# A two-layer hybrid attention network: the value products of four blocks of queries as one group on TensorE

## The chip, the cores and the metric

The kernel runs on one core of one Trainium2 chip. The metric is device time in microseconds of one execution, the median of several runs. The profile is one execution on the same kind of chip, recorded by the hardware profiler. PE is TensorE (matmuls and transposes), DVE is VectorE, ACT is ScalarE, POOL is GpSimd, SP is the engine whose queue issues most of the loads and stores.

## The reference, cut to what matters

The network has two layers over 2048 tokens of width 1024, in float32. The change lies in the second layer ("odd"), which has twelve heads of sliding-window attention with a sink, in three groups that share keys and values, and four heads that attend to a memory of 256 tokens. Each head has 64 features.

```python
def _sliding_window_attention(q, k, v, sinks):
    ...
    def one_block(bi):
        qi = lax.dynamic_slice_in_dim(q, bi * BLOCK, BLOCK, axis=1)
        kb = lax.dynamic_slice_in_dim(kp, bi * BLOCK, 2 * BLOCK, axis=1)
        vb = lax.dynamic_slice_in_dim(vp, bi * BLOCK, 2 * BLOCK, axis=1)
        s = jnp.einsum('bqhgd,bkhd->bhgqk', qi, kb, preferred_element_type=jnp.float32) * scale
        ...
        s = jnp.where(band, s, NEG_BIG)
        m = jnp.maximum(jnp.max(s, axis=-1, keepdims=True), sink)
        p = jnp.exp(s - m)
        w = p / (jnp.sum(p, axis=-1, keepdims=True) + jnp.exp(sink - m))
        return jnp.einsum('bhgqk,bkhd->bqhgd', w.astype(vb.dtype), vb)

def _odd_layer(x, mem, positions, w_in, w_memkv, sinks, w_out, ln_g, ln_b):
    ...
    mixed = jnp.concatenate([c_o, mem_o], axis=-1)
    y = (mixed * jax.nn.silu(gate)) @ w_out
    return _layer_norm(DEEPNORM_ALPHA * x + y, ln_g, ln_b)
```

BLOCK is 128: a block of 128 queries sees its own 128 keys and the 128 before them.

## The kernel before

The work runs in stages: the first layer's projections, its stick-breaking attention, its differential attention, the joining output projection and norm, the second layer's keys, values and gates (`layer2_kv`, `gates`), the second layer's queries and attention (`layer2`), and its output projection and norm (`out_proj`). The change lies in `layer2`.

There, features come in eight tiles `f` of 128 (two heads each; 0 to 5 are the sliding window's, 6 and 7 the memory's) and tokens in four chunks `t` of 512. A pair (f, t) is a chunk of work `i`, 32 in all; each has four blocks of 128 queries. One block of a chunk is a unit `u`, 128 in all. The loop over steps `u` writes several stages of different units side by side:

- the scores of unit u (`swa_scores` or `mem_scores`): four matmuls into a PSUM bank `z` (three of them). Behind them, off PE, comes the softmax: for the sliding window two DVE reductions that add the mask and take the maximum (L1143), a DVE copy of the sinks (L1145), two ACT exponentials with their sums (L1147), a DVE reciprocal (L1148), and the scaling of one head on DVE (L1154) and of the other on ACT (L1152). For the memory these are L484, L487, L489 and L493.
- a quarter of the projection of later queries, six matmuls of 512 columns (`fill`; `psmm`). The finished projection goes through ACT, DVE and POOL (L1116 to L1121, L1102, L1103) to become the next queries.
- the value products of unit u - 5 (`swa_values` or `mem_values`): four matmuls, each shown as two records of 128 by 64, that write a block's 128 columns of the one bank `pv`, the first head to its partitions 0 to 63 and the second to 64 to 127. After a chunk's fourth block DVE multiplies the bank by the chunk's gates (L1362), tile `sl`, and a store takes it to DRAM (`m2`).
- the four transposes of the softmax weights of unit u - 3 (`swa_turn`, `mem_turn`; `pstp`), which ACT or DVE copies from PSUM to a tile `wT` (L122, L124 in `evac`, through `tblocks`).

Only TensorE's instructions keep the order in which they are written (`PinnedCore(nc, self.tc, ("tensor",))`). What DVE, ACT, POOL and SP do, and in which order, is set by a planner that lays the program on a modelled timeline: each engine takes the earliest written instruction that is ready there. On the chip each queue is then kept in that order. A tag of a pool (`wT`, `sl`, `pv`) has a fixed number of buffers, and a new tile waits until the one that had its place is no longer used.

At the step's end, the loads of the next chunk's values and gates are written (`load_v`); keys and tables of angles come in the middle (`load_k`, `load_cs`). At chunk 29 the weights of the output projection are loaded and split in two parts (`load_wo`; L969 on ACT, L971 on POOL).

Line 56 is the helper that records every pinned instruction, so PE's instructions are told apart by their tiles; line 112 is the helper that issues loads and stores.

Of the kernel before, what the change touches and what calls it, by code (L numbers as in the profile page):

```python
# [15 lines left out]
S = 2048  # L16
D = 1024
P = 128
NB = S // P
TC = 512  # L20
# [25 lines left out]
class Pinned:  # L46
    """An engine whose instructions stay in the order in which they are written."""
# [18 lines left out]
class Net:  # L66
# [15 lines left out]
    @contextmanager  # L82
    def phase(self, bufs, banks, side="left"):
        """Pools for one phase; SBUF slots and PSUM banks by tag."""
        with ExitStack() as ctx:
            layer = {k: (n, ctx.enter_context(self.tc.tile_pool(name=self.nm("p" + k), bufs=1, side=side, reuse_waits="tile")))
                     for k, n in bufs.items()}
            if banks:
                ps = ctx.enter_context(self.tc.tile_pool(name=self.nm("pp"), bufs=1, space=bass.MemoryType.PSUM, reuse_waits="tile"))
                layer.update({"ps" + k: (n, ps) for k, n in banks.items()})  # L90
            self.layers.append(layer)
            yield
            self.layers.remove(layer)
# [20 lines left out]
    def turn(self, key, pattern):  # L114
        """The next letter of a repeated pattern: which engine takes this one."""
        k = self.turns.get(key, 0)
        self.turns[key] = k + 1
        return pattern[k % len(pattern)]
# [8 lines left out]
    def consts(self):  # L127
        nc, sb = self.nc, self.sb
# [4 lines left out]
        # nothing, then what is after the query (a column further on: at it or after it)  # L133
# [12 lines left out]
        # -lambda on every partition  # L146
# [26 lines left out]
    def rope_tables(self, k, sink):  # L173
        """cos and sin of the positions' angles, in chunks of 512: sink(chunk, cos, sin)."""
        nc = self.nc
        for t in range(NT):
            posi = self.t("c2", I32)
            self.dma(posi, self.i["pos"][t * TC:(t + 1) * TC].partition_broadcast(P))
            ang = self.t("c2")
            nc.vector.tensor_copy(ang, posi)  # L180
            nc.vector.tensor_scalar_mul(ang, ang, self.freq[:, k:k + 1])
            n = self.t("c2")
            nc.vector.tensor_scalar(n, ang, 1.0 / TWO_PI, MAGIC, ALU.mult, ALU.add)
            nc.vector.tensor_scalar_add(n, n, -MAGIC)
            for c in (C1, C2, C3):
                nc.vector.scalar_tensor_tensor(ang, n, -c, ang, ALU.mult, ALU.add)
            nc.vector.tensor_scalar(ang, ang, math.pi, -math.pi, ALU.min, ALU.max)
            nc.scalar.activation(n, ang, AF.Abs)
            sink(t, n, ang)
            yield  # L190

# [1 line left out]
    def wtile(self, src):  # L193
        """A [P, 8, 128] tile of weights, as two parts."""
        w, (fill,) = self.wtile_steps(src, 1, self.nc.gpsimd)
        fill()
        return w
# [21 lines left out]
    def load_x(self, between):  # L219
        """x transposed, [tc][half] -> (hi, lo) of [P, 4, 512]."""  # L220
        nc = self.nc
# [21 lines left out]
    def proj_t(self, w, t):  # L243
        """[128 features, 512 tokens] of chunk t."""
        return self.proj_side([w], t)[0]

    def proj_side(self, ws, t):
        """The same for several tiles of weights side by side."""
# [8 lines left out]
    def spill_parts(self, ps, dst, t, scale=None):  # L257
        """ps (times a power of two) in two parts to dst [2, P, S]."""
# [112 lines left out]
    def rope_all(self):  # L371
        """Both layers' tables to DRAM, a chunk of one at each next()."""
# [13 lines left out]
    def vtile(self, g):  # L386
        """Weights of 256 columns of the two attentions' values, as two parts of each half."""
# [9 lines left out]
    def values(self, g, ws, side):  # L397
        """256 columns of the two attentions' values, token by token."""
# [19 lines left out]
    def dup_parts(self, hi, lo, src, hh):  # L418
        """Half hh of src's partitions, its two parts in both halves of hi and lo."""
# [13 lines left out]
    def memkv(self, W, mem, keep):  # L433
        """Memory keys of each pair of heads and all values, a weight tile at each next()."""
# [35 lines left out]
    def tblocks(self, blocks, pattern="AV"):  # L470
        """Up to four [P, P] blocks transposed, in SBUF."""
# [8 lines left out]
    def softmax_pair(self, z, e, n0, sink=False):  # L480
        """z [P, 2, 256] -> e, normalised; columns from n0 on; the first is the sink's."""
# [13 lines left out]
    def mem_scores(self, qs, qcol, mk):  # L495
        """One block of queries, heads 2f and 2f+1 over the memory."""
# [20 lines left out]
    def load_qstack(self, src, t):  # L517
        """[P = two copies of 64, 2 heads, 2 parts, 512]."""
# [9 lines left out]
    def load_sb(self, p):  # L528
        """A pair of heads' keys and values and the last chunk's queries."""
# [69 lines left out]
    def differential(self):  # L599
        """Differential attention in three stages, each a unit (two blocks of queries, 17 blocks of  # L600
        keys together, of two heads) behind the one before: scores and exponentials; the mix of the
        two softmaxes; the product with the values. Between them go some feature tiles' share of
        the output projection."""
# [10 lines left out]
        def mixed(a, b):  # L614
            """Two lists evenly mixed, each in its order."""
            order = sorted([((i + 0.5) / len(a), 0, i) for i in range(len(a))] + [((i + 0.5) / len(b), 1, i) for i in range(len(b))])
            return [(a, b)[k][i] for _, k, i in order]
# [56 lines left out]
    def load_dq(self, p, k, h):  # L674
        """Queries of a half of each of the two chunks: units j = 2h and 2h + 1."""
# [7 lines left out]
    def diff_parts(self, unit):  # L683
        """Of the two blocks of queries: their number, the chunk's, the place in it, the keys, the
        first column in a row."""
# [4 lines left out]
    def diff_scores(self, unit, rows):  # L690
        """For each head and component the steps of its scores, and those of the exponentials."""
# [56 lines left out]
    def diff_mix(self, unit, rows):  # L748
        """Steps by beat."""
# [72 lines left out]
    def diff_norm(self, p, t, s0, pv, tail):  # L822
        """rms norm over each head's 64, scaled by the first sum; the rest of its steps to tail."""
# [42 lines left out]
    def filler(self):  # L866
        """alpha x and the share of the output projection of the feature tiles known before the
        differential attention; lists of steps."""
# [60 lines left out]
    def memory(self, mk, mv):  # L929
        """The first layer's attention over the memory, a block at each next(), to go  # L930
        between other projections."""
# [52 lines left out]
    def out_proj(self, w, msrc, spans, res, alpha, lng, lnb, tbs, ahead):  # L984
        """A block of the output projection and its layer norm at each next()."""
# [50 lines left out]
    def join(self, tail):  # L1036
        """The rest of the first layer's output projection, its norm, x of the second layer
        transposed in two parts, and its first gates; the steps in tail go between."""
# [60 lines left out]
    def qstack_head(self, qs, src, hh, eng):  # L1099
        """The two parts of head hh's queries (half of src's partitions), one on top of the other."""  # L1100
# [4 lines left out]
    def qstack_from(self, src, eng):  # L1105
        """[P = two parts of 64, 2 heads, 512] of a tile of two heads' queries (in SBUF)."""
# [22 lines left out]
    def swa_scores(self, qb, head, qs, qcol, ks):  # L1129
        """Heads head and head+1 over a block of keys and the one before; the first  # L1130
        column of that one is out of every query's window and takes the sink."""
# [37 lines left out]
    def gates(self, W, dst, om=None, m1=None, order=None, ws=None):  # L1169
        """silu of the gates to dst; times what has been attended to m1 where that is known."""  # L1170
# [27 lines left out]
    def layer2_kv(self):  # L1198
        """Keys in two parts and values of each group, to DRAM."""
# [35 lines left out]
    def layer2(self):  # L1235
        """The projections of queries go in quarters between the blocks of the attention, whose
        three stages lie a block or two apart."""
# [3 lines left out]
        wts, qss, sls, es, wTs, pvs, ks, vs, out = {}, {}, {}, {}, {}, {}, {}, {}, []  # L1241
# [94 lines left out]
        for u in range(128 + 5):  # L1336
# [13 lines left out]
            if u >= 5:  # L1350
                i, qi = (u - 5) // 4, (u - 5) % 4
                f, t = order[i]
                if qi == 0:
                    pvs[i] = self.psum("pv")
                if f < 6:
                    v = {t_: vs.get((f, t_)) for t_ in (t - 1, t)}
                    self.swa_values(4 * t + qi, wTs.pop(u - 5), cols[qi], v, pvs[i])
                else:
                    self.mem_values(wTs.pop(u - 5), cols[qi], vs[f], pvs[i])
                if qi == 3:  # L1360
                    mt = sls.pop(i)
                    nc.vector.tensor_mul(mt, pvs.pop(i), mt)  # L1362
                    self.dma(self.m2[f, :, t * TC:(t + 1) * TC], mt, nc.scalar if i > 29 else None)
# [8 lines left out]
    def run(self):  # L1372
# [11 lines left out]
        with self.phase({"c2": 3, "sl": 2}, {}):  # L1384
# [4 lines left out]
            with self.phase({"big": 16}, {}):  # L1389
# [7 lines left out]
                with self.phase({"w": 4, "raw": 1, "cs": 2, "e": 4, "wT": 4, "kc": 2, "qs": 2, "vg": 4},  # L1397
# [78 lines left out]
```

## Time and profile before

| | |
|---|---|
| median of 3 runs | 2660.3 us (2658.35 to 2661.22) |
| the profiled execution (span from first to last instruction) | 2665.1 us |
| PE busy | 2503.5 us, 94% of the span |
| DVE busy | 1656.7 us, 62% |
| ACT busy | 1264.2 us, 47% |
| POOL busy | 1189.9 us, 45% |
| value products of layer 2 (`pspv<-wT,vg`), PE | 1000 records, 83.0 us busy in all |
| steps of the loop in `layer2` | from about 2075 to 2482.6 us of the span |

The profile has no time of the profiled execution but its span, 2665.1 us; that stands 4.8 us over the median of the runs. Matmuls overlap, and their ends are modelled, so a length of a PE row is no cost; the distance from one group's start to the next one's start is.

### The profile page before, as it was taken

What the parts mean: (1) busy time and instruction counts of PE and PEld (TensorE: products, weight loads), DVE (VectorE), ACT (ScalarE), POOL (GpSimd) and SP (SyncE); (2) the same over time, 40 slices, a digit from 0 to 9 for tenths busy, and PEclk for the clock granted to TensorE, in tenths of its full rate; (3) what the DMA queues carried; (4) which work ended last, traced back from release to release, by engine and by line L of the source; (5) the groups of instructions that cost most, each with busy time, mean ns of one, the idle gap of its engine ahead of it and who ended that gap; (6) DMA issues with size and microseconds to landing.
All of it is one profiled execution on the core that took longest, in us unless ns stands there. A gap on an engine that the chain in (4) does not pass through costs nothing. (4 is left out here: it accounts for less than half of the span.)

```text
span 2665.1 us, 42634 instructions
## 1 busy us (share of the span) xinstructions
PE 2503.5 (94%) x15564; PEld 1964.7 (74%) x15564; DVE 1656.7 (62%) x3672; ACT 1264.2 (47%) x2653; POOL 1189.9 (45%) x848
## 2 busy tenths in 40 slices
PE   9899999999989999968877988999999999999998
PEld 7788998888757777646655666678788777777887
DVE  5732223421379999888889878788321667677554
ACT  4532222221167777555665765744121677776200
POOL 1301004730056666465646746764541555535333
PEclk9999999999989999989988988999999999999999
DMA  7643223321842331442523422265332555532541
GB/s 273 212 146 125 70 88 105 137 103 52 203 104 70 82 71 34 99 116 73 127 78 95 108 76 74 70 215 173 88 101 75 162 154 162 152 96 99 194 147 67
DMA packets 199250, 311.60 MB, mean 117 GB/s; under 512 B 17921, under 2 KB 97281, under 8 KB 198529
## 3 DMA queue, kind: packets, MB, share of 16 engines
q1 hardware_dynamic: 198464, 307.83, 39.3%
q8 instruction: 123, 2.02, 0.3%
q10 hardware_dynamic: 576, 1.05, 0.1%
q14 instruction: 87, 0.70, 0.1%
HBM read 204.74 MB, written 104.07 MB: 116 GB/s over the span
## 5 line engine op out<-in xcount | busy, mean ns | idle before, releaser
L56 PE MATMUL psmm<-big,w 128*128 128x512 f32 x1680 | 415.4, 395 | 0.0
L56 PEld LDWEIGHTS psmm<-big,w 128*128 128x128 f32 x1680 | 306.8, 189 | 58.3
L586 POOL TENSOR_TENSOR wb<-wb,row 128x512 f32<-128x512 f32 (+3 forms) x192 | 219.5, 1154 | 136.4 <-DVE row L582 126.9
L582 DVE TENSOR_TENSOR_SCAN row<-psz,row,zero 128x512 f32<-128x512 f32 (+5 forms) x240 | 258.5, 1107 | 31.9 <-ACT psz L579 31.6
L253 PE MATMUL psmm<-big,w 128*128 128x512 f32 x1200 | 275.2, 389 | 0.0
L253 PEld LDWEIGHTS psmm<-big,w 128*128 128x128 f32 x1200 | 225.0, 188 | 47.0 <-issue 0.2
L56 ACT ACTIVATE row<-row,mn 128x2048 f32<-128x2048 f32 (+7 forms) x192 | 229.7, 1201 | 33.6 <-DVE mn L731 33.0
L56 PE MATMUL psmm<-big,mp 128*128 128x512 f32 x1056 | 244.5, 392 | 0.0
L725 DVE TENSOR_SCALAR_CACHE_REDUCE row<-psz 128x512 f32<-128x512 f32 (+1 forms) x324 | 200.9, 640 | 58.4 <-PE psz L56 55.9
L56 PEld LDWEIGHTS psmm<-big,mp 128*128 128x128 f32 x1056 | 198.3, 189 | 41.3 <-issue 0.3
L56 ACT COPY wT<-pstp 128x512 f32<-128x512 f32 (+3 forms) x240 | 121.4, 522 | 169.8 <-PE pstp L56 163.0
L1190 DVE TENSOR_TENSOR c<-psmm,c 128x512 f32<-128x512 f32 x62 | 42.6, 691 | 240.3 <-ACT c L1189 240.3
L592 PE MATMUL pspv<-wT,kv 128*64 128x128 f32 x1632 | 158.1, 287 | 15.4 <-ACT wT L122 15.4
L771 POOL TENSOR_TENSOR row<-row,tiny 128x1536 f32<-128x1536 f32 (+3 forms) x48 | 132.9, 2769 | 83.9 <-DVE tiny L766 78.1
L772 POOL TENSOR_TENSOR row<-row,row 128x1536 f32<-128x1536 f32 (+3 forms) x48 | 163.3, 3408 | 1.9
L208 POOL TENSOR_TENSOR w<-w,w 128x1024 fp32r<-128x1024 f32 x20 | 48.8, 2440 | 255.8 <-ACT w L207 155.4
L56 PE MATMUL psmm<-wo,mp 128*128 128x512 f32 x480 | 155.3, 437 | 3.1 <-ACT mp L56 2.3
L578 ACT ACTIVATE wb<-psz 128x512 f32<-128x512 f32 (+3 forms) x240 | 129.9, 541 | 53.6 <-PE pstp L475 37.2
L778 DVE SCALAR_TENSOR_TENSOR row<-row,tiny,row 128x128 f32<-128x128 f32 (+7 forms) x72 | 153.2, 2154 | 0.5
L573 PE MATMUL psz<-kv,qs 128*128 128x512 f32 (+3 forms) x480 | 150.0, 406 | 2.1 <-DVE row L582 2.0
L592 PEld LDWEIGHTS pspv<-wT,kv 128*64 128x64 f32 x1632 | 106.7, 139 | 60.5 <-issue 20.5
L56 PE MATMUL pstp<-ident,row 128*128 128x128 f32 x816 | 142.0, 297 | 9.7 <-DVE c L860 8.1
(222 smaller groups left out, 5241.6 us busy)
## 6 DMA issues: line engine op xcount, KB each, us to landing
silu<-c SPq DMA_DIRECT2D x54, 256.0 KB, 2.3
sl<-silu SPq DMA_DIRECT2D x54, 256.0 KB, 3.3
qs<-sbq SPq DMA_DIRECT2D x48, 256.0 KB, 5.3
cs<-rope SPq DMA_DIRECT2D x24, 512.0 KB, 4.4
kc<-k SPq DMA_DIRECT2D x36, 320.0 KB, 5.1
w<-in_we_dram SPq DMA_DIRECT2D x20, 512.0 KB, 3.7
raw<-in_wo_dram SPq DMA_DIRECT2D x20, 512.0 KB, 4.0
rx<-in_x_dram SPq DMA_DIRECT2D x32, 256.0 KB, 2.7
```

What stands on the lines that cost most here:

```text
L56: return self.tc.keep_in_program_order(f(*a, **k))
L208: eng.tensor_sub(lo[:, sl], raw[:, sl], hi[:, sl].bitcast(F32))
L253: self.nc.tensor.matmul(ps, w[a][:, c, :], self.xpart(t, c, b), start=(c == k == 0), stop=(c == 7 and k == 2))
L573: nc.tensor.matmul(z[:, :m], qs[:, hh, k, qcol], ks[hh][:, lo:hi], start=(k == 0), stop=(k == 1 and not diag))
L578: nc.scalar.activation(w[:, :m], z[:, :m], AF.Sigmoid, scale=0.125)
L582: nc.vector.tensor_tensor_scan(prr[:, lo + s0 - 1:hi - 1][:, ::-1], z[:, s0:m][:, ::-1], self.zero.to_broadcast([P, m - s0]), prr[:, hi - ...
L586: eng.tensor_mul(w[:, :m], w[:, :m], prr[:, lo:hi])
L592: nc.tensor.matmul(pv[64 * hh:64 * hh + 64, qcol], vp[:, blk, 64 * hh:64 * hh + 64], wT[hh][:, j * P:(j + 1) * P], start=(hi == n and j == ...
L725: nc.vector.tensor_scalar(e[:, col + lo:col + lo + n0], z[:, :n0], -scale, before, ALU.mult, ALU.min, accum_out=acc)
L771: self.nc.gpsimd.tensor_mul(y[:, a:n], y[:, a:n], cf[hh][:, :1].to_broadcast([P, n - a]))
L772: self.nc.gpsimd.tensor_add(x[:, a:n], x[:, a:n], y[:, a:n])
L778: self.nc.vector.scalar_tensor_tensor(x[:, lo:hi], y[:, lo:hi], cf[hh][:, w:w + 1], x[:, lo:hi], ALU.mult, ALU.add)
```

## The change

A chunk's value products are no longer written block by block at four steps, one behind another. They are written together, at every fourth step: at step u, a multiple of four from 8 on, all 16 matmuls (12 where the chunk's first block has half of them) of chunk (u - 8) / 4, that is of units u - 8 to u - 5, then at once the product with the gates and the store. These stood at the same step before. The pool of transposed weights has six tiles and not four, the pool of gates (which the first layer's differential attention uses too) three and not two, and the scratch that is set aside for DMA descriptors is given a size of 2048. The rest of the diff takes out comments and descriptions, at unchanged line numbers.

```diff
-            if u >= 5:
-                i, qi = (u - 5) // 4, (u - 5) % 4
+            if u >= 8 and u % 4 == 0:
+                i = (u - 8) // 4
                 f, t = order[i]
-                if qi == 0:
-                    pvs[i] = self.psum("pv")
-                if f < 6:
-                    v = {t_: vs.get((f, t_)) for t_ in (t - 1, t)}
-                    self.swa_values(4 * t + qi, wTs.pop(u - 5), cols[qi], v, pvs[i])
-                else:
-                    self.mem_values(wTs.pop(u - 5), cols[qi], vs[f], pvs[i])
-                if qi == 3:
-                    mt = sls.pop(i)
-                    nc.vector.tensor_mul(mt, pvs.pop(i), mt)
-                    self.dma(self.m2[f, :, t * TC:(t + 1) * TC], mt, nc.scalar if i > 29 else None)
+                pv = self.psum("pv")
+                for qi in range(4):
+                    if f < 6:
+                        v = {t_: vs.get((f, t_)) for t_ in (t - 1, t)}
+                        self.swa_values(4 * t + qi, wTs.pop(4 * i + qi), cols[qi], v, pv)
+                    else:
+                        self.mem_values(wTs.pop(4 * i + qi), cols[qi], vs[f], pv)
+                mt = sls.pop(i)
+                nc.vector.tensor_mul(mt, pv, mt)
+                self.dma(self.m2[f, :, t * TC:(t + 1) * TC], mt, nc.scalar if i > 29 else None)
...
-        with self.phase({"c2": 3, "sl": 2}, {}):
+        with self.phase({"c2": 3, "sl": 3}, {}):
...
-                with self.phase({"w": 4, "raw": 1, "cs": 2, "e": 4, "wT": 4, "kc": 2, "qs": 2, "vg": 4},
+                with self.phase({"w": 4, "raw": 1, "cs": 2, "e": 4, "wT": 6, "kc": 2, "qs": 2, "vg": 4},
                                 {"mm": 2, "z": 3, "tp": 2, "pv": 1}):
...
-    nc = _bacc.Bacc("TRN2", target_bir_lowering=False, num_devices=1)
+    nc = _bacc.Bacc("TRN2", target_bir_lowering=False, num_devices=1, dynamic_dma_scratch_size=2048)
```

More of the change, by code (lines that the diff above doesn't have):

```diff
@@ L1240, in layer2 @@
         W = self.i["wo"]
-        wts, qss, sls, es, wTs, pvs, ks, vs, out = {}, {}, {}, {}, {}, {}, {}, {}, []
+        wts, qss, sls, es, wTs, ks, vs, out = {}, {}, {}, {}, {}, {}, {}, []
         order = [(f, t) for f in range(7) for t in range(NT)] + [(7, t) for t in (3, 0, 1, 2)]
```

## The prediction

> **What bounds the kernel now.** First the page's span, then the busy table of the second layer's attention (stretch, length, each engine's busy us and instructions, granted clock, DMA share, GB/s).
>
> ```profile
> span 2665.1 us, 42634 instructions
> ```
>
> ```profile
> core 0: us, PE busy (x) PEld busy (x) DVE busy (x) ACT busy (x) POOL busy (x), PEclk, DMA share, GB/s
> 2093.57:2376.84 283.27, 273.78 (x1961) 208.29 (x1959) 198.81 (x814) 208.57 (x584) 156.13 (x117) 1.00 0.54 150
> 2376.84:2433.78 56.94, 53.81 (x387) 41.24 (x386) 43.08 (x99) 40.65 (x112) 27.72 (x16) 1.00 0.34 114
> 2433.78:2482.62 48.84, 48.64 (x366) 37.18 (x366) 33.32 (x79) 30.34 (x82) 10.32 (x7) 0.97 0.23 71
> ```
>
> The changed code runs from 2093.57 to 2482.62: first the sliding-window heads (96 units of one block of queries, two heads), then, from 2376.84, the memory heads (32 units). PE is shown busy 274 of 283 us there, which looks like a PE bound. The groups of that stretch, here up to 2378.12 (line, engine, tiles, count | busy us, mean ns | idle before it, and who ended that) say otherwise:
>
> ```profile
> L1147 ACT ACTIVATE e<-e,tiny 128x256 f32<-128x256 f32 (+1 forms) x180 | 88.9, 495 | 55.5 <-DVE e L1145 54.9
> L1143 DVE CUSTOM_DVE_ANT_0 e<-psz,mask,nsink 128x256 f32<-128x256 f32 (+1 forms) x181 | 78.7, 472 | 0.0
> L1145 DVE COPY e<-nsink 128x2 f32<-128x2 f32 x90 | 36.6, 412 | 0.0
> L124 DVE COPY wT<-pstp 128x512 f32<-128x512 f32 (+1 forms) x31 | 20.7, 668 | 9.8 <-PE pstp L56 9.2
> L1148 DVE RECIPROCAL tiny<-tiny 128x2 f32<-128x2 f32 x91 | 14.9, 164 | 62.0 <-ACT e L1147 61.0
> ```
>
> DVE's reduction of the scores (L1143) stands idle 0.0 us before its 181 instructions: it never waits for PE's scores. What waits is DVE for ACT's exponentials (62.0 us before L1148) and ACT for DVE (55.5 us before L1147). One turn of that loop, DVE then ACT:
>
> ```profile
> 2218.27 0.16 DVE L1145 COPY e<-nsink 128x2 f32<-128x2 f32 x1
> 2219.59 0.17 DVE L1148 RECIPROCAL tiny<-tiny 128x2 f32<-128x2 f32 x1 [1.16 <-ACT e L1147]
> 2219.68 0.48 DVE L1143 CUSTOM_DVE_ANT_0 e<-psz,mask,nsink 128x256 f32<-128x256 f32 x1
> 2220.49 0.35 DVE L1154 TENSOR_SCALAR e<-e,tiny 128x256 f32<-128x256 f32 x1
> ```
>
> ```profile
> 2218.47 0.51 ACT L1147 ACTIVATE e<-e,tiny 128x256 f32<-128x256 f32 x1 [0.56 <-DVE e L1145]
> 2219.37 0.19 ACT L1147 ACTIVATION_READ_ACCUMULATOR e<-e,tiny 128x1 f32 x1
> ```
>
> The planner put unit u's reciprocal (L1148) ahead of unit u+1's reduction on DVE's queue, so the two engines take turns: the copy ends at 2218.43, the exponentials run 2218.47 to 2219.56, the reciprocal starts at 2219.59, the next reduction at 2219.68. The 181 reductions, two a unit, fill the 284.6 us of this view: the softmax loop takes 284.6 / 90.5 = 3.14 us a unit. PE, as the next PE view shows, needs 3.04 us a step. The two are nearly level, and the loop is the slower. In the memory heads (the last two stretches) it is PE that has next to no idle time, but for one stall, below.
>
> **The change, part by part.** PE's rows (start, length with overlap, tiles, count), first an ordinary step, then the last step before any value product, then a step whose first block has half the products:
>
> ```profile
> 2119.68 0.72 PE L56 MATMUL psz<-kc,qs 128*128 128x256 f32 x4
> 2120.24 1.55 PE L56 MATMUL psmm<-big,w 128*128 128x512 f32 x6
> 2121.71 0.66 PE L56 MATMUL pspv<-wT,vg 128*64 128x128 f32 x8
> 2122.30 0.66 PE L56 MATMUL pstp<-ident,e 128*128 128x128 f32 x4
> 2122.72 0.72 PE L56 MATMUL psz<-kc,qs 128*128 128x256 f32 x4
> ...
> 2090.03 1.55 PE L56 MATMUL psmm<-big,w 128*128 128x512 f32 x6
> 2091.42 0.60 PE L56 MATMUL pstp<-ident,e 128*128 128x128 f32 x4
> 2091.77 0.71 PE L56 MATMUL psz<-kc,qs 128*128 128x256 f32 x4
> ...
> 2142.71 0.44 PE L56 MATMUL pspv<-wT,vg 128*64 128x128 f32 x4
> 2143.08 0.66 PE L56 MATMUL pstp<-ident,e 128*128 128x128 f32 x4
> ```
>
> From start to start: scores 0.56, projection 1.47, products 0.59, transposes 0.42, together 3.04. Without products the projection takes 1.39 and the transposes 0.35, so a step is 2.30 and the products cost 0.74. Four records take 0.37 and eight 0.59: 0.055 a record, 0.44 for eight. So 0.30 of the 0.74 is spent on going from 128-column to 64-column tiles and back. Four groups now cost 4 x 0.74 = 2.96; one group of 32 costs 32 x 0.055 + 0.30 = 2.06. **The change takes 0.90 us of PE time from each chunk**: 28.8 us over 32 chunks, 2.815 us a step on average. No instruction is added or removed.
>
> The page "TensorEngine Tiling (Array Packing)" of the Trainium skill (section Key Properties) states that a change of tiling mode, not merely of tile, drains TensorE. The trace agrees on the sign, with its 0.30 us; if PE alone set the time, this rule would make the whole 28.8 us a gain, about 2631; that is the first rival below, priced there from the rows.
>
> *Sliding-window stretch.* The saving falls on an engine that isn't last: the loop sets the end, so its direct worth is 0. What the loop can get is DVE's own waits for PE. The table of waits for this stretch (who for whom: us, times, longest):
>
> ```profile
> DVE wT L124 <- PE pstp L56: 9.0, 9, 1.7
> DVE sl L1362 <- PE pspv L56: 5.4, 9, 1.4
> POOL w L208 <- DMA sl<-silu: 1.7, 1, 1.7
> ```
>
> The first two are 14.4 us in 18 waits, 0.8 each. In the turn above DVE would have waited 1.16 for ACT anyway, of which an evacuation of 0.67 (L124) leaves 0.49 as cover; about 18 x 0.3 = 5.5 us are exposed. Three of four steps become earlier and the fourth later: I take half, **2.8**, bounds 0 and 5.5.
>
> *The stall at the memory heads.* DVE, then PE:
>
> ```profile
> 2431.08 1.95 DVE L493 TENSOR_SCALAR e<-e,tiny 128x256 f32<-128x256 f32 x2
> 2432.95 0.68 DVE L1362 TENSOR_TENSOR sl<-pspv,sl 128x512 f32<-128x512 f32 x1
> 2433.78 0.82 PE L56 MATMUL pspv<-wT,vg 128*64 128x128 f32 x8 [3.13 <-DVE sl L1362]
> ```
>
> There is one bank for the products. Before, the next chunk's first products come one step behind the last ones, and here the product with the gates (L1362) is late, since DVE's queue ahead of it waits for ACT. With the change the next group comes four steps later, 4 x 2.30 = 9 us, so this wait of 3.1 goes. So does the half clock behind it: 0.97 over 48.84 us is 0.03 x 48.84 = 1.5. Together **4.6**. What is late next: L493's weights of the softmax, ready at 2433.03. Their transposes come one step behind the stalled one, now at about 2433.78 + 0.59 + 3.04 + 1.5 = 2438.9, so PE can gain 5.9 there at most, and 4.6 are already counted: the 0.90 of each of the four chunks between 2377 and 2434 is taken at 0 (bounds 0 and 3.6).
>
> *After it* PE is busy 48.64 of 48.84 us: four whole groups (chunks 27 to 30) save 4 x 0.90 = **3.6**. The last chunk's products now all stand behind the last transposes:
>
> ```profile
> 2480.60 0.66 PE L56 MATMUL pstp<-ident,e 128*128 128x128 f32 x4
> 2481.18 0.66 PE L56 MATMUL pspv<-wT,vg 128*64 128x128 f32 x8
> 2482.04 0.66 PE L56 MATMUL pspv<-wT,vg 128*64 128x128 f32 x8 [0.20 <-DVE wT L124]
> 2482.62 1.19 PE L56 MATMUL psmm<-big,mp 128*128 128x512 f32 x4
> ```
>
> From those transposes to the output projection are 2.02 us now. With the change two groups of 0.59 that stand ahead of them are gone (1.2 earlier), but behind them PE waits for the evacuation (2482.04 - 2480.60 = 1.44) and only then has 32 records of 0.055 and the switch back, some 1.9: 1.44 + 1.9 - 2.02 - 1.2 = 0.1 longer. I take **-0.2**, bounds -0.7 and 0.
>
> *The rest, at nothing.* Two more transposed-weight tiles: at most five are alive ahead of a group (blocks u-8 to u-4), the sixth is a spare; with four the group would wait for itself. A third gate tile lets its load start before the old one is stored; in this stage no PE instruction waits for such a load. The outer pool also serves the first layer's differential attention, with no count of instructions changed; I bound a shift of the order there at 1.7 either way, by the one wait for such a load in the table above (POOL's L208). The smaller scratch for DMA descriptors makes room; every load goes by the same queues as before. The group adds a wait: all PE work of the step stands behind the newest of its four tiles, the same tile and lag as now.
>
> Sum: 2.8 + 4.6 + 3.6 - 0.2 = 10.8. The profiled execution's span of 2665.1 becomes 2654.3; it stands 4.8 above the median 2660.3 of the runs, so the runs would show **2649.5**.
>
> **The rivals.** *The loop loosens (2624).* With scores 2.30 apart in three of four steps, the planner could put the next reduction ahead of the reciprocal, and DVE would reduce while ACT exponentiates. For it: DVE is busy 198.81 and ACT 208.57 of 283.27, which both fit PE's 90.5 x 2.815 = 254.8. Then the stretch takes PE's time, 28.5 less, and with the 8.0 behind it 36.5 come off. Against it, the start of the stage, where scores come 1.87 us apart and DVE still waits for the reciprocal first:
>
> ```profile
> 2084.41 0.64 PE L56 MATMUL psz<-kc,qs 128*128 128x256 f32 x4
> 2086.28 0.64 PE L56 MATMUL psz<-kc,qs 128*128 128x256 f32 x4
> ```
>
> ```profile
> 2086.42 0.17 DVE L1148 RECIPROCAL tiny<-tiny 128x2 f32<-128x2 f32 x1 [1.16 <-ACT e L1147]
> 2086.51 0.48 DVE L1143 CUSTOM_DVE_ANT_0 e<-psz,mask,nsink 128x256 f32<-128x256 f32 x1
> ```
>
> *The long step holds the loop (2678).* The fourth step grows to 2.30 + 2.06 = 4.36, 1.3 longer than now, and its transposes come 1.3 late. Their evacuation stands in DVE's or ACT's queue between parts of the loop. On DVE (one in three) 0.49 is covered, on ACT nothing: (0.8 + 2 x 1.3) / 3 = 1.13, times 23 chunks, 26 us, less the 8 outside the loop: +18. For it: DVE waits 9.2 us for transposes already. Against it: the planner sees the long step too and may place the evacuation behind it. It decides where more than a third of the evacuations stay in place.
>
> *No difference (2660).* The memory heads' gain is taken again by DVE and ACT, busy 43.08 and 40.65 of 56.94 there, in another order; for it the wait of L1362, which was DVE's and not PE's; against it PE's 48.64 of 48.84.
>
> One cost of the loop hangs on the order alone and may go either way in each of these cases: L1145 takes 0.16 in the turn above, but 0.412 on average, so 90 x 0.25 = 22 us of the stretch are waits inside that copy. The page "SBUF — State Buffer" of the Trainium skill (Who interferes with whom) states that DVE copies in a two-port mode and GpSimd instructions lock each other out for a whole instruction; the trace has the waits, and POOL busy 156.13 of 283.27, and by that rule which copies are hit depends on what POOL runs just then.
>
> **How the numbers follow.** Forecast 0.45 (its own range 2641 to 2656), loosened loop 0.22, long step 0.16, no difference 0.17. A measurement of this kernel tells about 0.2%, 5.3 us. Faster: the loosened loop and nearly all of the forecast, 0.64; within: 0.20; slower: 0.16. The range takes in most of the loosened loop (low 2621) and the long step at half its price, +9 (high 2669).
>
> **What would show it.** Right: groups of 32 product records every fourth step, 2.06 us from start to start with the switch; the steps between at 2.30 where PE doesn't wait; reductions (L1143) still idle 0.0 and the reciprocal still waiting for ACT some 60 us; PE's idle time ahead of the transposes (it waits there for DVE's weights) grown by 15 us or more; the sliding-window stretch 278 to 283 us long; no 3 us wait at the products and no half clock there. Wrong: that stretch near 255, or longer than 290; a wait for L1362 that stays; a difference ahead of 2060 us, in the first layer, larger than 2 us.

## The result and the profile after

The changed kernel takes **2677.6 us** (median of four runs, 2673.3 to 2686.1) beside 2660.0 for the kernel before: a ratio of 1.0073 [1.0054, 1.0092]. It is 0.7% slower, where 2649.5 was forecast, with 2669 as the upper end. One of the six executions of `e1_pools`, further down, took 3072.0 us at a mean granted clock of 0.744, where every other execution here has 0.968 or more, and is left out of its ratio.

The profiled execution of the changed kernel, span and first table:

```profile
span 2673.3 us, 42662 instructions
PE 2479.5 (93%) x15564; PEld 1967.2 (74%) x15564; DVE 1657.2 (62%) x3672; ACT 1267.0 (47%) x2653; POOL 1189.6 (44%) x848
```

PE's busy time fell by 24 us (2503.5 to 2479.5), with the same number of matmuls, while the time rose. So PE does have less to do, and the time was lost elsewhere. The busy table of the changed stage, cut at the same points as before (first the sliding-window heads, then the memory heads up to the output projection):

```profile
core 0: us, PE busy (x) PEld busy (x) DVE busy (x) ACT busy (x) POOL busy (x), PEclk, DMA share, GB/s
2092.80:2388.85 296.05, 260.88 (x1936) 210.97 (x1935) 203.31 (x814) 210.08 (x584) 154.68 (x117) 0.99 0.51 142
2388.85:2490.85 102.00, 97.37 (x778) 81.46 (x776) 74.06 (x176) 71.35 (x195) 40.21 (x24) 0.98 0.29 98
```

Sliding window: 283.27 us before, 296.05 now, PE busy 12.9 us less and idle 25.7 us more. Memory heads: 105.78 before (56.94 + 48.84), 102.00 now. Cut a little later, at the last sliding-window reduction, the same two read 287.9 to 301.2 (+13.3) and 101.1 to 96.8 (-4.3): the attention stage, from its first scores to the output projection, went **from 403.9 to 412.9 us**. These last figures, and the like of them below, are distances between single rows of the traces: unit 4's first reduction, the last reduction, the first `psmm<-big,mp`. What follows the stage is 182.5 us in both traces. The stages ahead of it can't be compared from one trace each: they vary by more from one execution to the next than the change could move them (last section).

The groups of the sliding-window stretch (2092.8 to 2391) in the changed kernel; the columns are those of the prediction's table of groups:

```profile
L1147 ACT ACTIVATE e<-e,tiny 128x256 f32<-128x256 f32 (+1 forms) x180 | 89.2, 497 | 62.0 <-DVE e L1145 61.7
L1143 DVE CUSTOM_DVE_ANT_0 e<-psz,mask,nsink 128x256 f32<-128x256 f32 (+1 forms) x181 | 78.7, 472 | 0.0
L56 PE MATMUL pstp<-ident,e 128*128 128x128 f32 x354 | 56.6, 281 | 35.1 <-DVE e L1145 18.5 <-DVE e L1154 15.5 <-ACT c L1116 0.6
L1154 DVE TENSOR_SCALAR e<-e,tiny 128x256 f32<-128x256 f32 x90 | 48.8, 542 | 0.0
L1145 DVE COPY e<-nsink 128x2 f32<-128x2 f32 x90 | 37.1, 412 | 0.0
L124 DVE COPY wT<-pstp 128x512 f32<-128x512 f32 (+1 forms) x31 | 20.7, 668 | 8.3 <-PE pstp L56 8.2
L1118 DVE STREAM_SHUFFLE c<-c 128x512 f32<-128x512 f32 x21 | 15.4, 736 | 0.1
L1148 DVE RECIPROCAL tiny<-tiny 128x2 f32<-128x2 f32 x91 | 15.0, 165 | 79.1 <-ACT e L1147 78.3
L1361 DVE TENSOR_TENSOR sl<-pspv,sl 128x512 f32<-128x512 f32 x22 | 15.0, 682 | 1.1 <-PE pspv L56 1.1
```

The reductions (L1143) still never wait. DVE waits for ACT's exponentials 79.1 us (62.0 before), ACT for DVE 62.0 us (55.5 before), and PE waits 35.1 us at the transposes for DVE's scaled weights. The turn-taking loop of DVE and ACT still sets the time of the stretch, and it has become **longer**: 3.16 to 3.31 us a unit (287.9 and 301.2 over 91 units).

What lengthened it shows in DVE's rows. First a turn of the changed kernel, then one of the kernel before at its product with the gates:

```profile
2169.05 0.48 DVE L1143 CUSTOM_DVE_ANT_0 e<-psz,mask,nsink 128x256 f32<-128x256 f32 x1
2169.45 1.23 DVE L1154 TENSOR_SCALAR e<-e,tiny 128x256 f32<-128x256 f32 x1
2170.60 0.68 DVE L1361 TENSOR_TENSOR sl<-pspv,sl 128x512 f32<-128x512 f32 x1
2171.20 0.72 DVE L1145 COPY e<-nsink 128x2 f32<-128x2 f32 x1
```

```profile
2227.23 0.35 DVE L1154 TENSOR_SCALAR e<-e,tiny 128x256 f32<-128x256 f32 x1
2227.49 0.16 DVE L1145 COPY e<-nsink 128x2 f32<-128x2 f32 x1
2227.60 0.69 DVE L1362 TENSOR_TENSOR sl<-pspv,sl 128x512 f32<-128x512 f32 x1
2229.42 0.17 DVE L1148 RECIPROCAL tiny<-tiny 128x2 f32<-128x2 f32 x1 [1.14 <-ACT e L1147]
```

ACT's row that waits for that copy in the changed kernel:

```profile
2171.96 0.51 ACT L1147 ACTIVATE e<-e,tiny 128x256 f32<-128x256 f32 x1 [1.13 <-DVE e L1145]
```

Before, the product with the gates (0.69 us) stands behind the copy of the sinks, in the time in which DVE waits for ACT anyway. Now it stands ahead of the copy, and ACT, which needs the copy, waits 1.13 us. Not all of that wait is the product's: in this turn the scaling (L1154) took 1.23 us and the copy 0.72, where the turn of the kernel before has 0.35 and 0.16. The order of DVE's queue over the sliding-window units, counted: between a unit's reductions and its copy stood before 0 products with the gates, 5 shuffles (L1118) and 6 evacuations (L124); now **13 products, 14 shuffles and 8 evacuations**. At their mean lengths of 0.68, 0.74 and 0.67 us that is 8.8 + 6.7 + 1.3 = 16.8 us more in the loop. The loop's legs, as means over the 86 units in which the copy follows the reductions (us, from starts and ends of the rows):

| | before | after | after, order held (`e2_after_behind`) |
|---|---|---|---|
| first reduction to the copy's end | 1.705 | 1.911 | 1.581 |
| copy's end to the exponentials | 0.261 | 0.253 | 0.316 |
| exponentials | 1.093 | 1.096 | 1.094 |
| their end to the reciprocal | 0.094 | 0.046 | 0.032 |
| reciprocal to the next reduction | 0.090 | 0.091 | 0.092 |
| a turn | 3.242 | 3.397 | 3.115 |

The first leg grew by 0.206, 17.7 us over 86 units; the fourth gave 4.1 back; together 13.3, which is what the stretch lost. Taken from start to start of DVE's rows, the 17.7 us of the first leg are 15.1 of the three kinds (7.8 products, 5.6 shuffles, 1.7 evacuations) and 4.6 of a longer scaling, less 2.1 of a shorter copy. The scaling's group before the change, beside its 542 ns above:

```profile
L1154 DVE TENSOR_SCALAR e<-e,tiny 128x256 f32<-128x256 f32 x90 | 43.0, 478 | 0.0
```

So the order of the queue makes up most of the loss, and DVE's longer scaling a smaller part. What lengthened the scaling was not tested.

### The profile page after: what moved, and what is told of

The parts are those of the page before. It is cut to its first block, busy times and chain, and to the rows that moved or that the text cites. A ratio compares the mean times of both kernels' runs of the same rounds, so it can differ in the third digit from the quotient of the medians.

```text
span 2673.3 us, 42662 instructions
## 1 busy us (share of the span) xinstructions
PE 2479.5 (93%) x15564; PEld 1967.2 (74%) x15564; DVE 1657.2 (62%) x3672; ACT 1267.0 (47%) x2653; POOL 1189.6 (44%) x848
## 5 line engine op out<-in xcount | busy, mean ns | idle before, releaser
L56 ACT ACTIVATE row<-row,mn 128x2048 f32<-128x2048 f32 (+7 forms) x192 | 229.9, 1202 | 37.2 <-DVE mn L731 36.5
```

The source lines that it names most:

```text
L56: return self.tc.keep_in_program_order(f(*a, **k))
```

## The experiments

Each kernel was compared with the kernel before in rounds on the same chip. "Attention" is the stage's length in the trace, as above (before 403.9, after 412.9).

### The change again, and its pools alone

`e0_after` is the changed kernel as it stands.

> The changed kernel once more, beside the others on the same chip. Theory P (place on DVE's queue): in the sliding-window stretch the planner now puts 13 gate products, 14 shuffles and 8 evacuations between a unit's reductions and its copy of the sinks, where nothing covers them; before it was 0, 5 and 6. (13 x 0.69) + (9 x 0.74) + (2 x 0.67) = 17 us. Theory L (long step): PE's step of 32 products makes the transposes late, and DVE and ACT wait for them. Both expect about 2675, with single runs between 2670 and 2686.

Measured: 1.006 [1.0047, 1.0073], 2676.4 us; attention 411.9. The result stands.

`e1_pools` is the kernel before with the three sizes and nothing else:

```diff
-        with self.phase({"c2": 3, "sl": 2}, {}):
+        with self.phase({"c2": 3, "sl": 3}, {}):
...
-                with self.phase({"w": 4, ..., "wT": 4, ...},
+                with self.phase({"w": 4, ..., "wT": 6, ...},
...
-    nc = _bacc.Bacc("TRN2", target_bir_lowering=False, num_devices=1)
+    nc = _bacc.Bacc("TRN2", target_bir_lowering=False, num_devices=1, dynamic_dma_scratch_size=2048)
```

> The kernel before with the three pool sizes of the change (three gate tiles, six tiles of transposed weights, the smaller DMA scratch), value products block by block as before. Theories P and L both expect 2660 within 0.2%, since DVE's order is that of before. Rival S: the sizes or the new addresses cost the time; then about 2675.

Measured: **1.0040 [1.0027, 1.0053]**, 10.6 us slower, with an attention stage of 403.8, the same as before. What follows the stage is as long as before, too (182.5 us). So some 10.6 us of the loss [7.2, 14.1], more than half by the middle value, are not in the changed loop at all: the sizes cost them, ahead of the attention. With the stage's own 9.0 that makes 19.6 us, beside 17.7 measured.

### The order of DVE's queue, held

`e2_after_behind` is the changed kernel with a rule for the planner: products with the gates, shuffles and evacuations go on DVE's queue behind the newest copy of the sinks. `e3_before_behind` is the kernel before with the same rule. The edit, with the dependency's arguments and the unchanged lines shortened to dots:

```diff
+    def behind_copy(self, ins):
+        if getattr(self, "sinks", None) is not None:
+            self.tc.add_manual_dep(ins.ins, self.sinks.ins.name, ...NoSync...)
...
-            self.nc.vector.tensor_copy(out, in_)
+            self.behind_copy(self.nc.vector.tensor_copy(out, in_))
...
-        nc.vector.stream_shuffle(sw[:n], q[:n], SHUF_S)
+        self.behind_copy(nc.vector.stream_shuffle(sw[:n], q[:n], SHUF_S))
...
-        nc.vector.tensor_copy(e[:, :, ns], self.nsink[:, head:head + 2])
+        self.sinks = nc.vector.tensor_copy(e[:, :, ns], self.nsink[:, head:head + 2])
...
-                nc.vector.tensor_mul(mt, pv, mt)
+                self.behind_copy(nc.vector.tensor_mul(mt, pv, mt))
```

> The changed kernel with one addition: on DVE's queue a gate product, a shuffle or an evacuation of the second layer's attention may not stand ahead of the newest unit's copy of the sinks. All 22 products, 22 shuffles and 30 evacuations of that stretch then stand behind the copy, under ACT's exponentials (1.1 us). Theory P: the 17 us come back and some more, since 25 us of such work stand ahead of the copy now: 2650 to 2660. Theory L: PE's long step is as before and its transposes as late, so 2670 or more.

> The kernel before with the same rule for DVE's queue; there only 5 gate products and 2 evacuations are left ahead of the copy (before the rule 6 evacuations and 5 shuffles). Theory P: about the same as before, 2652 to 2662, so that grouping the products under the same rule is worth little or nothing as long as the softmax loop sets the time. Theory L: 2660, and the grouped kernel under the rule 10 or more above it.

Measured: e2 0.9990 [0.9978, 1.0002], 2657.2 us, attention **392.3**; e3 1.0012 [1.0003, 1.0021], 2661.4 us, attention 407.2. The stretch of e2 and three of its groups (this file's lines stand five further down: L1148 is the reduction, L1150 the copy, L1153 the reciprocal):

```profile
2099.42:2381.55 282.13, 263.31 (x1985) 216.35 (x1984) 196.66 (x829) 213.81 (x595) 157.58 (x118) 0.99 0.56 151
```

```profile
L1148 DVE CUSTOM_DVE_ANT_0 e<-psz,mask,nsink 128x256 f32<-128x256 f32 (+1 forms) x184 | 80.0, 472 | 0.0
L1150 DVE COPY e<-nsink 128x2 f32<-128x2 f32 x91 | 29.6, 328 | 0.0
L1153 DVE RECIPROCAL tiny<-tiny 128x2 f32<-128x2 f32 x92 | 15.3, 166 | 86.6 <-ACT e L1152 86.6
```

None of the three kinds stands ahead of the copy now, the stretch is 282.1 us and not 301.2, and the whole stage is 20.6 us shorter than the changed kernel's, with PE's order untouched. The loop is still closed: reductions 0.0, reciprocal 86.6. So the order of DVE's queue is what the grouping lost its time to. The rule moved one thing more: the copy itself became shorter (0.412 to 0.328 us on average). Of the 28.4 us that the first leg lost against the changed kernel over its 86 turns, 21.4 are the three kinds and 7.5 the copy, while the scaling took 0.6 more. The three kinds alone are more than the 13.3 that the stretch had lost.

In e3 the rule helped next to nothing in the loop (286.5 us beside 287.9): it took 6.3 us of these kinds out of the first leg, and there the scaling became 9.6 us longer and the copy 4.1 shorter. Its memory heads took 105.9 us beside 101.1, for a reason that was not looked into. With the rule on both sides, the grouping gains 407.2 - 392.3 = 14.9 us, of which 4.4 lie in the sliding-window stretch and 10.5 in the memory heads. Which of the three kinds costs most was not run apart.

### The loop opened

`e4_after_unlock` and `e5_before_unlock` write a unit's reciprocal, memset and scalings one step later and keep the reciprocal at that place, so that DVE reduces the next unit while ACT exponentiates this one.

```diff
-        nc.vector.reciprocal(r, s)
-        nc.vector.memset(e[:, :, ns], 0.0)
-        for hh in range(2):
...
-        return e
+        def rest():
+            self.tc.keep_in_program_order(nc.vector.reciprocal(r, s))
+            nc.vector.memset(e[:, :, ns], 0.0)
+            for hh in range(2):
...
+        return e, rest
...
-                    es[u] = self.swa_scores(4 * t + qi, 2 * f, qss[i], cols[qi], ks[f, t])
+                    es[u], left = self.swa_scores(4 * t + qi, 2 * f, qss[i], cols[qi], ks[f, t])
+                    if u:
+                        rest()
+                    rest = left
...
```

> The changed kernel with the softmax loop opened: in the sliding-window heads a unit's reciprocal and scaling are written one step later, and the reciprocal stands behind the next unit's copy of the sinks on DVE's queue, so that DVE reduces the next unit while ACT exponentiates. Theory P with the saving of 0.90 us a chunk on PE: PE becomes the bound, 2.82 us a step; the attention stage, 412 us from its first scores to the output projection in the changed kernel, falls by 30 to 40; 2635 to 2647. Rival: the engines' own work or the latency from scores to weights binds at the old pace; then 2665 or more.

> The kernel before with the same opened loop. Theory P: PE binds at 3.04 us a step, 9 us less than the loop's pace over the stretch: 2645 to 2655, and the grouped kernel's attention stage is shorter than this one's by 20 to 29 us (0.90 x 32 at most). Rival: the grouping saves PE nothing that can be used; then both stages are alike within 5 us.

Measured: e4 **0.9890 [0.9875, 0.9905]**, 2633.6 us, attention 371.0; e5 0.9974 [0.9963, 0.9985], 2653.7 us, attention 397.3. In time e4 came out just below the 2635 to 2647 expected, e5 inside its 2645 to 2655. The busy row of e4's stretch (columns as above) and its groups (its reciprocal is L1149), then e5's reductions:

```profile
2091.09:2351.09 260.00, 254.54 (x1948) 214.70 (x1948) 246.90 (x827) 204.56 (x591) 158.06 (x118) 1.00 0.59 162
```

```profile
L1143 DVE CUSTOM_DVE_ANT_0 e<-psz,mask,nsink 128x256 f32<-128x256 f32 (+1 forms) x184 | 79.5, 468 | 0.0
L56 PE MATMUL pstp<-ident,e 128*128 128x128 f32 x354 | 55.3, 277 | 4.1 <-ACT wT L122 4.1
L1149 DVE RECIPROCAL tiny<-tiny 128x2 f32<-128x2 f32 x91 | 14.1, 155 | 0.4 <-ACT e L1147 0.4
```

```profile
L1143 DVE CUSTOM_DVE_ANT_0 e<-psz,mask,nsink 128x256 f32<-128x256 f32 (+1 forms) x184 | 79.6, 469 | 15.1 <-PE psz L56 7.1 <-PE psmm L56 6.4 <-issue 1.4
```

The reciprocal's wait for ACT falls from 79.1 to 0.4 us, PE's idle time at the transposes from 35.1 to 4.1. With the loop open the pace is close to PE's in both: in e5 the reductions wait for it for the first time (15.1 us), and the stretch takes 279.3 / 91 = 3.07 us a unit, beside the 3.04 of PE's step that the prediction read off; in e4 it takes 260.0 / 91 = 2.86, beside 2.815, and PE stands idle 5.5 us of the 260.0. There the reductions still never wait, and DVE is busy 246.9 us, so DVE is not far behind. The grouping, which cost 9.0 us of the stage with the loop closed and DVE's order free, is worth 397.3 - 371.0 = **26.3 us** once it is open (19.3 in the sliding-window stretch, 7.0 in the memory heads), of 28.8 that PE saves. The rule of the Trainium skill that a change of tiling mode drains TensorE ("TensorEngine Tiling (Array Packing)", Key Properties) agrees with that: the same matmuls with a quarter of the changes took 26.3 us less.

e4's PE rows over a long and a short step:

```profile
2202.77 0.72 PE L56 MATMUL psz<-kc,qs 128*128 128x256 f32 x4
2203.32 1.56 PE L56 MATMUL psmm<-big,w 128*128 128x512 f32 x6
2204.81 1.97 PE L56 MATMUL pspv<-wT,vg 128*64 128x128 f32 x32
2206.71 0.66 PE L56 MATMUL pstp<-ident,e 128*128 128x128 f32 x4
2207.12 0.72 PE L56 MATMUL psz<-kc,qs 128*128 128x256 f32 x4
...
2209.42 0.72 PE L56 MATMUL psz<-kc,qs 128*128 128x256 f32 x4
```

The long step is 2207.12 - 2202.77 = 4.35 us (4.36 forecast), the short one 2.30 (2.30): the group costs 2.05 beside the 2.06 worked out.

### Which of the sizes

Kernel before with the smaller scratch alone (`e6_scratch`); with the scratch and the third gate tile (`e10_scratch_sl`); with the scratch and six `wT` (`e11_scratch_wt`); and the changed kernel with two gate tiles (`e12_after_sl2`). The edits are the single lines of e1's diff; that of e12 is

```diff
-        with self.phase({"c2": 3, "sl": 3}, {}):
+        with self.phase({"c2": 3, "sl": 2}, {}):
```

> The kernel before with the smaller DMA scratch alone. With the room it gives, three loads of output-projection weights (256 KB each) no longer wait for a place and the planner puts them ahead of the first loads of x on SP's queue. Theory Q: these loads at the head delay PE's start by 3 to 4 us and the rest of the pools' 10 us follows from it or from the third gate tile; 2661 to 2670. Rival: the 10 us of the pool sizes are the third gate tile's (other order of loads in the differential attention); then 2656 to 2661 here.

> The kernel before with the smaller scratch and three gate tiles. The three pool sizes together cost 0.4% (10 us), the scratch alone 0.07%. Theory G: it is the third gate tile, which lets the gate loads of the first layer's differential attention move ahead of other loads on SP's queue; 2666 to 2672 beside 2658 to 2662 for the kernel before. Rival W: it is the six tiles of transposed weights; then this is within 0.15% of before.

> The kernel before with the smaller scratch and six tiles of transposed weights. Theory G: like the scratch alone, within 0.2% of before. Rival W: 2666 or more.

> The changed kernel with two gate tiles as before; the order on DVE's queue is that of the changed kernel to the last instruction. Theories P and G: the 9 us of the sliding-window stretch stay, the 8 us of the third gate tile go: 2665 to 2671. If the third tile costs nothing, 2673 or more; if the place on DVE's queue costs nothing, 2663 or less.

| | ratio to before | attention, us |
|---|---|---|
| e6: scratch | 1.0007 [0.9996, 1.0017] | 404.2 |
| e11: scratch, `wT` 6 | 1.0014 [1.0003, 1.0026] | 404.3 |
| e10: scratch, `sl` 3 | 1.0028 [1.0017, 1.0040] | 403.9 |
| e1: all three | 1.0040 [1.0027, 1.0053] | 403.8 |
| e0: the change | 1.0060 [1.0047, 1.0073] | 411.9 |
| e12: the change, `sl` 2 | 1.0044 [1.0028, 1.0061] | 411.7 |

The third gate tile is the largest part by these figures: 0.21% on the kernel before (e10 against e6), 0.16% on the changed one (e0 against e12), some 5 us. It is not measured well. Taken together, the two intervals leave 0.05 to 0.37% for the first difference, and for the second, from -0.05 to 0.37%, they can't tell it from nothing. The whole 8 us that was expected to go in e12 (2665 to 2671) did not: it took 2672.2. The scratch and the `wT` tiles have 0.07% each, which these intervals can't tell from nothing. No gain stands against the gate tile: the attention stage is as long with two as with three. Where ahead of the attention the 5 us go was not settled: no stage's length differs between the traces by more than it does between executions of the same sizes.

One place was tested. With the smaller scratch, three loads of 256 KB stand second in SP's queue, ahead of the first x; SP's rows behind its first load in the changed kernel, then in the kernel before:

```profile
1.17 1.37 SPq L112 DMA_DIRECT2D rx<-in_woute_dram  x3
2.58 0.43 SPq L56 DMA_DIRECT2D w<-in_xT_dram  x1
```

```profile
1.16 0.42 SPq L56 DMA_DIRECT2D w<-in_xT_dram  x1
```

`e7_scratch_hold` has the smaller scratch and keeps these loads behind the last load of x, which it remembers as `xload`:

```diff
-            self.dma(raws[k], i["woute"][tiles[k], :, 512 * h:512 * h + 512])
+            ld = self.dma(raws[k], i["woute"][tiles[k], :, 512 * h:512 * h + 512])
+            self.tc.add_manual_dep(ld.ins, self.xload.ins.name, ...NoSync...)
...
```

> As the kernel with the smaller scratch alone, but these three loads may not stand ahead of the last load of x on SP's queue; they come some 40 loads later. Theory Q: the start is that of before, and the time is 2656 to 2661. If the addresses or the scratch itself cost the time, it stays where the scratch alone puts it.

Measured: 1.0006 [0.9998, 1.0015], 2662.9 us beside 2661.9 for the kernel before on that chip, as e6. That these early loads cost the time is not borne out; there may be nothing of the scratch's to explain.

### The parts that help, together

`e13_best` is the changed kernel with the loop opened as in e4, two gate tiles as in e12, and the three loads held as in e7.

> Grouped products with the opened softmax loop, two gate tiles, six tiles of transposed weights, and the three weight loads held behind x. The grouped kernel with the opened loop took 2633.6. Theory G: 8 us less, 2622 to 2630. If the third gate tile costs nothing: 2630 to 2636.

Measured: **0.9872 [0.9850, 0.9893]**, 2627.1 us, attention 370.7. It is 1.3% faster than the kernel before and has the lowest time of all, but its interval overlaps e4's [0.9875, 0.9905], so that the two gate tiles and the held loads are not shown to add anything to the opened loop.

## Why the prediction was wrong

**Right: what binds, and what PE saves.** The loop of DVE and ACT, not PE, sets the sliding-window stretch (0.0 us idle ahead of L1143 in both kernels; e4 and e5 opened it). PE's arithmetic held to 0.01 us on the steps shown (e4).

**The step that failed: "the loop sets the end, so its direct worth is 0", with 2.8 us for DVE's waits.** It measured 13.3 us lost. The waits that the 2.8 came from did shrink. The changed kernel's waits in the stretch (who for whom: us, times, longest):

```profile
PE pstp L56 <- DVE e L1145: 18.5, 22, 2.5
ACT wT L122 <- PE pstp L56: 8.6, 7, 1.6
DVE wT L124 <- PE pstp L56: 7.3, 10, 1.0
DVE sl L1361 <- PE pspv L56: 1.1, 2, 0.7
```

DVE waits 8.4 us for PE and not 14.4. What the step left out is that the loop's own length depends on what the planner puts into it, and that the planner lays every queue anew when PE's order changes. The prediction counted the loop as a fixed 3.14 us. It spoke of DVE's order only for the evacuations, in the rival of the long step, and for the waits inside the copy; these did not change in sum (L1145 takes 0.412 us on average in both), while the scaling, which it left out, went from 0.478 us to 0.542. The covered place, behind the copy, and the exposed one, ahead of it, lie within one turn, and 15 us of work moved from the one to the other. With the order held (e2 against the kernel before) the stage gains 11.7 us, 5.8 of them up to the last reduction, where 10.8 and 2.8 were forecast. Why the planner chose that order in its modelled time was not looked into.

**"The rest, at nothing" failed too.** The pool sizes and the scratch cost 10.6 us [7.2, 14.1] (e1), where 1.7 was the bound. That every load goes by the same queue as before is true and was no reason: their order on the queue changed. The third gate tile, about half of it by the middle values, gained nothing that shows. How the sizes cost the time stays open.

**The memory heads: 8.0 forecast (4.6 + 3.6 - 0.2), 4.3 measured.** The 3.1 us wait for L1362 went, as said. So did the half clock behind it. But PE's waits there came to 4.6 us in all, beside 3.3 before, so the term for the stall was mis-sized: it took the waits that would come in its place at nothing. What came late next was not the transposes for want of the softmax weights, as the prediction had it, but chiefly an evacuation:

```profile
2446.32 1.55 PE L56 MATMUL psmm<-big,w 128*128 128x512 f32 x6
2450.15 1.11 PE L56 MATMUL pstp<-ident,e 128*128 128x128 f32 x4 [2.28 <-ACT wT L122]
2450.92 1.20 PE L56 MATMUL psz<-kc,qs 128*128 128x256 f32 x4
2451.92 2.18 PE L56 MATMUL psmm<-big,w 128*128 128x512 f32 x6
```

PE waits 2.28 us for ACT's copy of the transposes, and the half clock comes behind this wait instead (six matmuls of the projection take 2.18 and not 1.55). ACT's copy stood behind exponentials that had waited 4.63 us for DVE's reduction (L484), which stood on DVE's queue behind the scaling of earlier weights (L493, 2.75 us).

**The rivals.** The long step had the right time, 2678, for another reason: it asked for 26 us of waits for the late transposes, and those of L124 and L122 together went from 10.6 (9.0 and 1.6) to 15.9. e2 keeps the long step and is level with the kernel before. The loosened loop (2624) did not come of itself: the planner kept the reciprocal ahead of the next reduction (0.09 us between them in the table of legs). Written into the code, it gave most of what it was priced at: the stage 32.9 us shorter in e4, 36.5 forecast.

**The signs named.** Right: groups of 32 records, steps of 2.30, reductions idle 0.0, no 3 us wait at the products, PE's idle time at the transposes up by more than 15 (8.8 to 35.1). Against it: the stretch of 296 us, over the 290 named as a sign of being wrong, and a half clock in the memory heads. A difference ahead of 2060 us was named as a sign, but one trace of each kernel can't show it: the first scores start at 2078.7 before and 2077.9 after, though the sizes cost 10 us.

## What to carry to other kernels

When two engines take turns and leave a third idle, the time hangs on what stands between the turns; a shorter neighbour is worth little, and a new order of the neighbour's work can put other instructions into the turn, where a planner lays out the queues. Before you cost such a change, look for the instructions that now lie in a covered place of the loop, price them in the exposed one, and open the loop first: the same regrouping cost this stage 9 us with the loop closed and gained 26 with it open. A buffer count or scratch size that "only makes room" is an edit of its own: run it alone.

## What the runs showed of the hardware

The first layer's differential stage (from the end of the stick-breaking scan to the first layer's norm) computes the same in every kernel here, with the same number of instructions on PE. It took 625.6 us in the trace of e3 and 636.7 in that of e2 (stretch, length, then the columns of the tables above):

```profile
1112.00:1737.60 625.60, 524.99 (x3534) 374.60 (x3533) 511.74 (x1408) 388.69 (x698) 378.36 (x150) 0.91 0.39 102
```

```profile
1113.80:1750.50 636.70, 530.87 (x3534) 379.23 (x3533) 514.34 (x1408) 388.68 (x698) 377.18 (x150) 0.90 0.38 100
```

The granted clock differs with it. By the trace's record of the granted clock, TensorE ran at half clock there for 112.6 us in e3, 119.5 in the changed kernel (629.9 us), 122.9 in the kernel before (633.2) and 126.3 in e2. e3 and the kernel before have two gate tiles, e2 and the changed kernel three, so each pair has the same sizes there, and within each pair the stage still differs (by 7.6 and 6.8 us). The half-clock times differ in steps of 3.4 us or twice that, which agrees with the window of about 3.4 us that the Trainium skill gives ("TensorE: Matmul & The Clock Gate", "The two states you'll see" in Part 1). Over 68 executions of the kernel before the same holds for the whole time: 11 with a mean granted clock under 0.9705 took 2665.0 us on average, 39 between that and 0.9725 took 2660.5, and 18 above it 2656.2. So a few half-clock windows, more or fewer from one execution to the next, go with most of the spread of this kernel. They need not be all of its cause: by an estimate from these figures, 13.7 us at half clock instead of full, as between e3 and e2, cost PE 6.9 of the 11.1 us at most. A single trace tells nothing of an edit worth 5 us that lies ahead of the attention.
